# Left sums kept on chip in place of the residual: twelve of sixteen v units by seven products, and probabilities scaled by ScalarE

## The chip, the core and the metric

The kernel runs on one core of a Trainium2 chip. The core has TensorE (PE, matmuls; the loading of its stationary operand is listed apart as PEld), VectorE (DVE), ScalarE (ACT), GpSimd (POOL) and SyncE (SP). Each engine carries out its own instructions in the order in which the program wrote them and waits for the others on semaphores. On-chip data lie in SBUF, matmul results in PSUM, which here is handed out as four pairs of banks. Transfers from and to the HBM are issued by SP, and some by POOL and ACT.

The metric is the device time of one execution in microseconds; lower is better. A line such as L1074 is a line of the kernel before.

## What is computed

A decoder of two layers for 256 tokens of 2048 channels, all in float32. Layer 0 is a pooling mixer and a convolutional feed-forward part. Layer 1 is an attention whose keys and values are computed from the stream after layer 0, and another feed-forward part. Each part is followed by a layer normalisation of a scaled residual plus the part's output. What the change touches is the attention of layer 1:

```python
k_shared = (h @ shared_w_k).reshape(B_, S, N_HEADS, HEAD_DIM)   # 16 heads of 128
v_shared = (h @ shared_w_v).reshape(B_, S, N_HEADS, HEAD_DIM)
q = (h @ w_q).reshape(B_, S, N_HEADS, HEAD_DIM)
# three causal dilated branches, merged by their softmax denominators
s = where(mask, q @ k.T / sqrt(Dh), NEG_INF)
pr = exp(s - m); den = sum(pr); o = pr @ v / den
mix = o.reshape(B_, S, D_MODEL) @ w_o
h = layer_norm(DEEPNORM_ALPHA * h + mix, ln1_g, ln1_b)
```

The kernel merges the three branches into one softmax in which the mask counts how many branches hold a key (`cnt`).

## The kernel before

**Weights as units.** The program is a list of units, each a weight block of 512 rows and up to 512 columns. `run_units` takes them in turn. Ahead of unit i it issues loads up to unit i+5 (`do_load`, on SP, into three raw buffers) and splits up to unit i+3 (`do_split`). A split writes the weight as a rounded part `wh` (ACT, L99) and a rest `wl` (DVE subtraction, L100), each in one of four buffers; products are then formed from the parts by three matmuls. After a unit's matmuls come the steps that were put off to it by `later(n, ...)`, and then the unit's own closing step. So the order of the instructions on ACT and DVE is: splits of unit i+3, steps put off to unit i, closing step of unit i.

**Eight or seven products.** A v unit in its normal form (`mk`, L255 to L257) multiplies 256 tokens by 512 rows by 512 columns with 24 matmuls of 512 columns. In the other form (`mk_seven`, L244 to L246) tokens, rows and columns are halved and seven products of halves take the place of eight (a Strassen-Winograd scheme). It is then two units, "a" with 18 and "b" with 24 matmuls of 256 columns. It needs sums of weight halves, which DVE forms in the raw buffer between the pieces of the split (`split_sums`: L120, L122, L124, with casts L119 and L113 on ACT and subtractions L121 and L114 on DVE), and sums of the halves of the left operand, the "left sums". For quarter j of the 2048 channels these are formed once by `v_sums(j)`: four DVE operations on the residual `H[j]` (L992 to L995) into a tile f, and one unit later a split of f by ACT and DVE (the lines L309 and L305). The weight halves' results are put together by `v_early` and `v_post`.

**Blocks.** The attention goes through four blocks of 512 columns (four heads each): for every block four units of k, four of q and four of v, where block 1 has its v ahead of its q. I write k0, q0, v0, k1, v1, q1 and so on, and j0 to j3 for the four quarters of channels, which are the units of a group. After v3 come the 16 units of the output projection (`add_last`). Which v units take seven products is written out in `v_group`: j3 in blocks 0 and 3, and j1 to j3 in blocks 1 and 2, eight in all.

**Scores.** When a q group ends, its result is brought to SBUF, and the steps of its block are put off by given numbers of units, two heads at a time. `scores`: two heads' scores on PE (L1055, L1056), on DVE the mask (L1059), the maximum (L1062, L1063), on ACT the exponential (L1066, four instructions), on DVE the multiplication by the counts with its sum (L1069), the reciprocal (L1071) and the scaling of the probabilities (L1074, four instructions). `blocks`: a transpose in 32x32 squares on DVE (L1080) into a tile `pb`, and one unit later 16 small DMAs, eight on SP and eight on POOL (L1093), which put the squares in their places (`pTs`). `outputs`: probabilities by v on PE (L1107, L1108) and the split of the result for the output projection (L1115, L1116).

**Buffers.** The pool `hp` has five buffers of 512 KB (tag "h"). The residual, which is wanted again after the output projection, holds four, `H[0]` to `H[3]`; the fifth serves `pb` and some others in turn. The pool `xcp` has seven buffers for split operands: the attention's input takes four, the rest are for the left sums of quarters 1 and 2 (`xsum`) and the attention's outputs (`oq`). The left sums of quarter 3 lie in small tiles here and there. A tile that finds all buffers of its tag taken waits until one is given up; the instruction that writes it waits with it, and the instructions behind that on its engine.

Of the kernel before, what the change touches and what calls it, by code (L numbers as in the profile page):

```python
# [9 lines left out]
F32 = mybir.dt.float32  # L10
F32R = mybir.dt.float32r
I32 = mybir.dt.int32
AF = mybir.ActivationFunctionType
OP = mybir.AluOpType
# [18 lines left out]
def trunk(ctx: ExitStack, tc: tile.TileContext, x, pool_w_in, pool_w_grp, pool_scale, pool_w_out,  # L33
# [267 lines left out]
    def quad_tile(nm):  # L301
        return xcp.tile([P, 4, 2, XW], F32R, name=nm, tag="xc")
# [662 lines left out]
        return vts[c][:, 0, :], vts[c][:, 1, :]  # L965

    def v_post(c):
        def post(t, ps):
            v = v_tile(c)[t]
            V.tensor_tensor(v, v, ps, OP.add)  # L970
        return post

# [9 lines left out]
        return early  # L982

    vsums = {}

    def v_sums(q, then):
        ap = pools["attn"]
        x = H[q]
        a11, a12, a21, a22 = (x[:, k::2, t * P:t * P + P] for k, t in ((0, 0), (1, 0), (0, 1), (1, 1)))
        f = hp.tile([P, 4, T], F32, name="f", tag="h") if q == 3 else ap.tile([P, 4, T], F32, name="f", tag="k")  # L990
        d = [f[:, i].rearrange("p (k t) -> p k t", k=2) for i in range(4)]
        V.tensor_tensor(d[0], a21, a22, OP.add)  # L992
        V.tensor_tensor(d[1], d[0], a11, OP.subtract)
        V.tensor_tensor(d[2], a21, a11, OP.subtract)
        V.tensor_tensor(d[3], a12, d[1], OP.subtract)  # L995

        def rest():
            if q < 3:
                t = quad_tile("xsum")
                vsums[q] = [[t[:, i, hl, :T].rearrange("p (k t) -> p k t", k=2) for hl in range(2)] for i in range(4)]  # L1000
                split_act(t, f)
                then()
                return
            w = w4("vs0").bitcast(F32R)
            z = ap.tile([P, 2, T], F32R, name="vs3", tag="vs3")
            vs = [[w[:, 0], w[:, 1]], [z[:, 0], z[:, 1]]]
            vs.append([lnp.tile([P, T], F32R, name=f"vs{nm}", tag=nm) for nm in ("S", "Q")])
            vs.append([w[:, 2], w[:, 3]])
            for i, v in enumerate(vs):
                A.copy(v[0], f[:, i])  # L1010
            for i, v in enumerate(vs):
                V.tensor_tensor(v[1], f[:, i], v[0].bitcast(F32), OP.subtract)
            vsums[q] = [[u.rearrange("p (k t) -> p k t", k=2) for u in v] for v in vs]
            then()

        later(1, rest)

    def qk_post(nm, hq):
# [3 lines left out]
        def evac(ps):  # L1022
# [9 lines left out]
                    A.copy(y, p[:, :, T:])  # L1032
                    V.tensor_tensor(y, y, p[:, :, :T], OP.add)
            if nm == "q":
                s0, b0, b1, o0, o1 = ((2, 4, 7, 8, 11), (2, 4, 7, 12, 14), (9, 11, 14, 15, 18), (2, 3, 5, 7, 8))[hq]
                later(s0, lambda: scores(hq, range(0, 2)))
                later(b0, lambda: blocks(hq, (0, 1)))
                later(s0 + 1, lambda: scores(hq, range(2, 4)))
# [2 lines left out]
                later(o1, lambda: outputs(hq, (2, 3)))  # L1041
                if hq == 0:
                    v_sums(3, lambda: None)
                    later(6, lambda: v_sums(1, lambda: v_sums(2, lambda: None)))
        return post

    def scores(hq, ms):
# [23 lines left out]
        V.reciprocal(mx[:, 0:2], mx[:, 4:6])  # L1071
        for h in range(2):
            for t, sl in parts:
                V.tensor_scalar(sf[:, h, sl], sf[:, h, sl], mx[:, t, h:h + 1], None, op0=OP.mult)  # L1074
        pr[hq, ms[0]] = two

    def blocks(hq, ms):
# [38 lines left out]
            V.tensor_tensor(o[:, :, 1, :T], both[:, :, :T], o[:, :, 0, :T].bitcast(F32), OP.subtract)  # L1116

    def v_group(hq):
        js = (0, 1, 2, 3)
        seven = {0: (3,), 1: (1, 2, 3), 2: (1, 2, 3), 3: (3,)}[hq]  # L1120
        group_tm(shared_w_v, rows4, 512 * hq, 512, xsrcs, v_post(hq),
                 seven={j: (lambda j=j: vsums[j]) for j in js if j in seven}, early=v_early(hq))

    for hq in range(4):
        x0 = hq == 0
# [3 lines left out]
        group(attn_w_q[0], rows4, 512 * hq, 512, xsrcs, qk_post("q", hq))  # L1129
        if hq != 1:  # L1130
            v_group(hq)
    add_last(attn_w_o[0], rows4, [lambda j=j: oq[j] for j in range(4)], True, 1, 0, after=to_tokens)
    marks.append(len(units))
    ffn(1)
# [139 lines left out]
```

## Time and profile before

| | us |
|---|---|
| runs | 2016.05, 2016.1, 2018.27 |
| median | 2016.1 |
| span of the profiled execution, first to last instruction | 2014.9 |
| busy in the span: PE / DVE / ACT | 2005.8 / 1734.9 / 1269.7 |
| share of the 16 DMA engines' time, main queue | 58.8% |

The profile gives no time of its own for what lies around the span of the profiled execution; the median of the runs is 1.2 us above it.

A line of the timeline gives the start in us from the span's start, the duration in us of the stretch of instructions, engine, line, operation, output and inputs, and the number of instructions; in square brackets stands how long the engine was idle ahead of it and what ended the wait. A line of the waits gives who waited for whom, and the total, the number and the longest of those waits. A line of the stretches begins with its bounds, and then has the busy time of the engines, each with its instructions, the granted clock of PE, the share of the DMA engines' time and the rate in GB/s. A line of the groups gives the instructions of one kind, their number, the busy time in us and the mean duration in ns. A line of the chain gives a start, a duration and what the end of the program waited for in that time. Matmuls overlap, so that the spacing of their starts and not their duration tells their price.

The attention's units run from 924 us (k0) to 1209 us (end of v3), and the output projection follows.

### The profile page before, as it was taken

Reading aid. Unit: us, or ns where it says so; the run is one execution under the profiler, and the core shown is the slowest. Engines: PE = TensorE matmul, PEld = TensorE weight load, DVE = VectorE, ACT = ScalarE, POOL = GpSimd, SP = SyncE. Lnnn points to the kernel's source line nnn. Section 1 sums busy time; section 2 is a strip of 40 time slices with the busy share of each in tenths; the row PEclk is TensorE's granted clock in tenths of the full one; section 3 lists DMA queues with packets and bytes.
Section 4 is the critical chain, followed back from the end, with each engine's and each line's share of the span. In section 5 each row is a group of like instructions: output and inputs, shape, how many; then the busy total and the mean of one; then the engine's idle time right before and its main releaser. Section 6 shows DMA issues by size and latency. Waiting matters only on the chain.

```text
span 2014.9 us, 31474 instructions
## 1 busy us (share of the span) xinstructions
PE 2005.8 (100%) x12760; PEld 1810.2 (90%) x12760; DVE 1734.9 (86%) x1831; ACT 1269.7 (63%) x1551; POOL 93.0 (5%) x153
## 2 busy tenths in 40 slices
PE   9999999999999999999999999999999999999999
PEld 8898988999899988889888988998899989989987
DVE  6868887999899899879896878787899899989899
ACT  6454686767766676657554445487766677667673
POOL 2000000000000000000001021000000000000000
PEclk9999999999999999999999999999999999999999
DMA  8565466666666757885465656557666756666765
GB/s 260 204 208 186 163 212 192 181 221 223 198 198 200 239 179 229 232 230 186 155 220 172 210 172 202 187 188 211 166 224 200 224 186 222 209 211 186 213 208 185
DMA packets 271297, 407.77 MB, mean 202 GB/s; under 512 B 74430, under 2 KB 85588, under 8 KB 270896
## 3 DMA queue, kind: packets, MB, share of 16 engines
q1 hardware_dynamic: 259488, 388.93, 58.8%
q0 software_dynamic: 11232, 16.18, 5.4%
q8 instruction: 100, 1.64, 0.3%
q10 hardware_dynamic: 432, 0.66, 0.1%
q14 instruction: 45, 0.37, 0.1%
HBM read 380.01 MB, written 2.10 MB: 190 GB/s over the span
## 4 chain that ended last, share of the span: by engine, by line
PE 88%; DVE 7%; ACT 2%; DMA 2%; issue 1%; SPq 0%; DVEq 0%; ACTq 0%
PE acc L180 41%; PE acc L181 21%; PE s L244 3%; PE s L246 3%; PE s L245 3%; PE acc L184 2%; PE acc L185 2%; PE acc L183 2%; PE t L246 2%; PE t L244 2%; PE t L245 2%; DVE wl L100 2%; ACT wh L99 1%; DVE wl L114 1%; DVE wl L121 1%
## 5 line engine op out<-in xcount | busy, mean ns | idle before, releaser
L180 PE MATMUL acc<-xc,wh 128*128 128x512 f32 x3264 | 1151.6, 396 | 0.0
L181 PE MATMUL acc<-xc,wl 128*128 128x256 f32 x3264 | 916.2, 281 | 0.8 <-DVE wl L100 0.8
L100 DVE TENSOR_TENSOR wl<-raw,wh 128x2048 fp32r<-128x2048 f32 (+2 forms) x304 | 654.8, 2162 | 171.0 <-ACT wh L99 163.3
L180 PEld LDWEIGHTS acc<-xc,wh 128*128 128x128 f32 x3264 | 616.1, 189 | 142.8 <-issue 0.4
L99 ACT CAST wh<-raw 128x2048 fp32r<-128x2048 f32 (+2 forms) x304 | 546.6, 1805 | 170.8 <-PE acc L180 65.7
L181 PEld LDWEIGHTS acc<-xc,wl 128*128 128x128 f32 x3264 | 615.2, 188 | 1.3 <-DVE wl L100 1.2
L113 ACT CAST wh<-raw 128x1024 fp32r<-128x1024 f32 x144 | 150.7, 1052 | 202.8 <-DVE raw L122 175.5
L114 DVE TENSOR_TENSOR wl<-raw,wh 128x1024 fp32r<-128x1024 f32 x144 | 171.8, 1221 | 11.2 <-ACT wh L113 11.2
L121 DVE TENSOR_TENSOR wl<-raw,wh 128x1536 fp32r<-128x1536 f32 x72 | 126.2, 1753 | 6.3 <-ACT wh L119 5.3
L119 ACT CAST wh<-raw 128x1536 fp32r<-128x1536 f32 x72 | 106.4, 1477 | 36.6 <-PE acc L180 26.5
L287 POOL DMA_DIRECT2D ht<-w x48 | 41.3, 1015 | 1446.4 <-DVE ht L873 720.9
L244 PE MATMUL t<-wh,g 128*128 128x256 f32 x376 | 105.8, 281 | 0.0
L246 PE MATMUL t<-wh,g 128*128 128x256 f32 x376 | 105.7, 281 | 0.0
L245 PE MATMUL t<-wl,g 128*128 128x256 f32 x376 | 105.5, 281 | 0.0
L616 ACT ACTIVATE c<-u,cv 128x256 f32<-128x256 f32 x172 | 89.5, 593 | 23.2 <-DVE f L678 16.5
L246 PE MATMUL s<-wh,xs 128*128 128x256 f32 x344 | 96.1, 279 | 0.0
L244 PE MATMUL s<-wh,xs 128*128 128x256 f32 x344 | 95.9, 279 | 0.0
L245 PE MATMUL s<-wl,xs 128*128 128x256 f32 x344 | 95.9, 279 | 0.0
L124 DVE TENSOR_TENSOR raw<-raw 128x1024 f32<-128x1024 f32 x72 | 88.2, 1225 | 2.4
L621 ACT ACTIVATE a<-u,cv 128x256 f32<-128x256 f32 x172 | 73.5, 500 | 11.9 <-DVE g L688 11.9
L607 ACT COPY u<-acc 128x512 f32<-128x512 f32 x84 | 46.8, 572 | 46.1 <-PE acc L181 45.9
L621 ACT ACTIVATE u<-u,cv 128x256 f32<-128x256 f32 x172 | 73.4, 500 | 0.0
(338 smaller groups left out, 3443.1 us busy)
## 6 DMA issues: line engine op xcount, KB each, us to landing
raw<-in_ffn_w_up_dram SPq DMA_DIRECT2D x160, 1024.0 KB, 5.2
raw<-in_ffn_w_down_dram SPq DMA_DIRECT2D x80, 1024.0 KB, 5.1
raw<-in_pool_w_out_dram SPq DMA_DIRECT2D x16, 1024.0 KB, 5.0
raw<-in_shared_w_k_dram SPq DMA_DIRECT2D x16, 1024.0 KB, 5.2
raw<-in_attn_w_q_dram SPq DMA_DIRECT2D x16, 1024.0 KB, 5.3
raw<-in_shared_w_v_dram SPq DMA_DIRECT2D x16, 1024.0 KB, 5.4
raw<-in_attn_w_o_dram SPq DMA_DIRECT2D x16, 1024.0 KB, 5.2
ht<-w POOLq DMA_DIRECT2D x50, 256.0 KB, 4.8
```

The lines of the kernel that those rows point to most:

```text
L99: A.copy(wh[i][:, s], r[:, s])
L100: V.tensor_tensor(wl[i][:, s], r[:, s], wh[i][:, s].bitcast(F32), OP.subtract)
L113: A.copy(h[:, :, n], r[:, :, n])
L114: V.tensor_tensor(l[:, :, n], r[:, :, n], h[:, :, n].bitcast(F32), OP.subtract)
L119: A.copy(hs, rs)
L121: V.tensor_tensor(ls, rs, hs.bitcast(F32), OP.subtract)
L180: PE.matmul(ps[m].ap, h[:, k, c], q[:, k, :, :T], start=st, stop=False)
L181: PE.matmul(ps[m][:, :T], l[:, k, c], q[:, k, 0, :T], start=False, stop=sp)
L244: PE.matmul(to, xh, h[:, k, n], start=opens and kk == 0, stop=False)
L245: PE.matmul(to, xh, l[:, k, n], start=False, stop=False)
L246: PE.matmul(to, xl, h[:, k, n], start=False, stop=ends and kk == 1)
L621: A.activation(to[:, m, :], u[:, m, i:i + T], AF.Copy, scale=cv[:, i, j:j + 1])
```

## The change

- The residual goes to HBM while the attention runs: four transfers out when q0 ends (`parked`), four back ahead of the first unit of the output projection (`back`).
- The four buffers thus given up hold the left sums of quarters 0 and 1, two each (rounded part and rest). Those of quarter 2 stay in `xcp`, those of quarter 3 where they were. `v_sums` is now formed for quarter 0 too, in the order 0, 1, 2, beginning one unit earlier.
- Seven products: j3 in block 0, all four in blocks 1 and 2, j0, j1 and j3 in block 3, twelve in all. Block 3 takes its quarters in the order 2, 0, 1, 3.
- `v_post` adds 256 columns where all four units of a group take seven products.
- The outputs of block 3 come two units later in the list, which has two more units there.
- The four scalings of the probabilities (L1074) go from DVE to ACT.

```diff
@@ v_post
-        def post(t, ps):
-            v = v_tile(c)[t]
+        def post(t, ps, half=0):
+            v = v_tile(c)[t][:, 256 * half:]
             V.tensor_tensor(v, v, ps, OP.add)
@@ before v_sums
+    aside = ctx.enter_context(tc.tile_pool(name="aside", bufs=1, space=bass.MemoryType.DRAM))
+    parked = [aside.tile([P, 4, T], F32, name=f"parked{c}") for c in range(4)]
+
+    def back():
+        for c in range(4):
+            H[c] = hp.tile([P, 4, T], F32, name="h", tag="h")
+            nc.sync.dma_start(H[c], parked[c])
@@ v_sums
             if q < 3:
-                t = quad_tile("xsum")
-                vsums[q] = [[t[:, i, hl, :T].rearrange("p (k t) -> p k t", k=2) for hl in range(2)] for i in range(4)]
-                split_act(t, f)
+                if q == 2:
+                    t = quad_tile("xsum")
+                    t = [t[:, :, hl, :T] for hl in range(2)]
+                else:
+                    t = [hp.tile([P, 4, T], F32R, name=f"xsum{hl}", tag="h") for hl in range(2)]
+                vsums[q] = [[u[:, i].rearrange("p (k t) -> p k t", k=2) for u in t] for i in range(4)]
+                A.copy(t[0], f)
+                V.tensor_tensor(t[1], f, t[0].bitcast(F32), OP.subtract)
                 then()
@@ qk_post
-                s0, b0, b1, o0, o1 = ((2, 4, 7, 8, 11), (2, 4, 7, 12, 14), (9, 11, 14, 15, 18), (2, 3, 5, 7, 8))[hq]
+                s0, b0, b1, o0, o1 = ((2, 4, 7, 8, 11), (2, 4, 7, 12, 14), (9, 11, 14, 15, 18), (2, 3, 5, 9, 10))[hq]
@@
                 if hq == 0:
                     v_sums(3, lambda: None)
-                    later(6, lambda: v_sums(1, lambda: v_sums(2, lambda: None)))
+                    for c in range(4):
+                        nc.sync.dma_start(parked[c], H[c])
+                    later(5, lambda: v_sums(0, lambda: v_sums(1, lambda: v_sums(2, lambda: None))))
@@ scores
             for t, sl in parts:
-                V.tensor_scalar(sf[:, h, sl], sf[:, h, sl], mx[:, t, h:h + 1], None, op0=OP.mult)
+                A.activation(sf[:, h, sl], sf[:, h, sl], AF.Copy, scale=mx[:, t, h:h + 1])
@@ v_group
-        js = (0, 1, 2, 3)
-        seven = {0: (3,), 1: (1, 2, 3), 2: (1, 2, 3), 3: (3,)}[hq]
-        group_tm(shared_w_v, rows4, 512 * hq, 512, xsrcs, v_post(hq),
-                 seven={j: (lambda j=j: vsums[j]) for j in js if j in seven}, early=v_early(hq))
+        js = (2, 0, 1, 3) if hq == 3 else (0, 1, 2, 3)
+        seven = {0: (3,), 1: (0, 1, 2, 3), 2: (0, 1, 2, 3), 3: (0, 1, 3)}[hq]
+        group_tm(shared_w_v, [rows4[j] for j in js], 512 * hq, 512, [xsrcs[j] for j in js], v_post(hq),
+                 seven={i: (lambda j=j: vsums[j]) for i, j in enumerate(js) if j in seven}, early=v_early(hq))
@@ ahead of the output projection
+    before.setdefault(len(units), []).append(back)
     add_last(attn_w_o[0], rows4, [lambda j=j: oq[j] for j in range(4)], True, 1, 0, after=to_tokens)
```

## The prediction

> **What bounds the kernel now.** I read the head of the page, then the waits of the run, then the attention stage by stretches.
>
> ```profile
> span 2014.9 us, 31474 instructions
> PE 2005.8 (100%) x12760; PEld 1810.2 (90%) x12760; DVE 1734.9 (86%) x1831; ACT 1269.7 (63%) x1551; POOL 93.0 (5%) x153
> PE acc L183 <- ACT wh L99: 1.6, 1, 1.6
> PE acc L181 <- DVE wl L100: 0.8, 1, 0.8
> ```
>
> PE has matmuls in flight in all but 9 us, and no wait of it is longer than 1.6 us: a microsecond taken from its work is won, a microsecond it must wait is lost. Its one wait in attention is the 0.8 us. Its place, and the busy time of the engines in four stretches (PE, PEld, DVE, ACT, POOL, then clock and DMA):
>
> ```profile
> 1041.19 0.38 PE L181 MATMUL acc<-xc,wl 128*128 128x256 f32 x1 [0.84 <-DVE wl L100]
> ...
> 969.08:1041.13 72.05, 71.27 (x432) 63.15 (x430) 69.23 (x98) 39.69 (x42) 9.11 (x16) 1.00 0.54 163
> 1041.13:1111.28 70.15, 70.09 (x399) 61.33 (x400) 50.75 (x65) 30.04 (x28) 8.95 (x16) 1.00 0.63 199
> 1111.28:1134.34 23.06, 23.06 (x169) 21.76 (x168) 19.62 (x18) 14.26 (x12) 0.08 (x1) 1.00 0.67 222
> ...
> 1183.23:1208.86 25.63, 25.63 (x141) 22.11 (x140) 19.81 (x39) 10.35 (x17) 2.98 (x6) 1.00 0.48 168
> ```
>
> The first stretch runs from late k0 to the first unit of q1 (block 0's v, k1, v1). DVE is busy 69.2 of its 72.05 us there, and at its end PE waits for DVE: DVE, not PE, sets that point, so what is added to DVE's row of work before it comes out at the end. Elsewhere DVE has slack.
>
> **What a seven saves.** The first matmuls of a normal v unit and of what follows it, then of a seven (a and b) and of what follows it:
>
> ```profile
> 1111.28 0.40 PE L255 MATMUL t<-wh,xc 128*128 128x512 f32 x1
> 1116.88 0.28 PE L244 MATMUL s<-wh,xc 128*128 128x256 f32 x1
> ...
> 1203.78 0.47 PE L244 MATMUL s<-wh,xc 128*128 128x256 f32 x1
> 1208.86 0.39 PE L180 MATMUL acc<-o,wh 128*128 128x512 f32 x1
> ```
>
> 5.60 against 5.08 us (42 matmuls at the spacing of 0.12 us): 0.5 us a unit, 2.1 us for four. That is all the change can take from PE.
>
> **Stage A, block 0's scores to q1: DVE gets longer.** First the scaling. DVE and ACT around the first scores of block 0:
>
> ```profile
> 986.26 1.50 ACT L1066 ACTIVATE p<-p,mx 128x128 f32<-128x128 f32 x4 [3.38 <-DVE mx L1063]
> 987.66 1.89 ACT L99 CAST wh<-raw 128x2048 fp32r<-128x2048 f32 x1
> ...
> 988.25 0.18 DVE L1071 RECIPROCAL mx<-mx 128x4 f32<-128x4 f32 x1
> 988.47 1.01 DVE L1074 TENSOR_SCALAR p<-p,mx 128x128 f32<-128x128 f32 x4
> 989.58 2.29 DVE L100 TENSOR_TENSOR wl<-raw,wh 128x2048 fp32r<-128x2048 f32 x1
> ...
> L621 ACT ACTIVATE a<-u,cv 128x256 f32<-128x256 f32 x172 | 73.5, 500 | 11.9 <-DVE g L688 11.9
> ```
>
> Now ACT casts the next weights (L99) while DVE finishes the scores, and DVE's subtraction starts as both are done, at 989.58. Each engine keeps the order of the program, and the four scalings stand ahead of that cast on ACT. They wait for the reciprocal (988.43). Their price on ACT is not in the trace: the exponentials, four of the same shapes, take 1.40 us from start to cast; four at L621's 0.50 (a copy with a scale from memory, twice the width of half of them) would be 2.0; DVE's own 1.01 is the low end. I take 1.40. Then the cast runs 989.85 to 991.75, and the subtraction behind it starts 2.2 us later than now; DVE idles meanwhile. Block 0 has two such calls: **+4.4 us**. A gain (the 1.1 us of L1074 twice) would need the cast ahead of the scalings.
>
> The Trainium skill, "ScalarE: Activation LUTs", section "Rules for kernel authors", gives multiplications to VectorE rather than ScalarE. The rows side with it (1.01 on DVE, 1.50 for ACT's four of those shapes), and by it alone the sum would lose only what ACT is slower; the order on ACT, which it does not speak of, is the larger part.
>
> Then the new left sums, and the seven of v1's first unit:
>
> ```profile
> 1007.66 0.42 DVE L992 TENSOR_TENSOR f<-h 128x256 f32<-128x256 f32 x1
> ...
> 1009.12 2.29 DVE L100 TENSOR_TENSOR wl<-raw,wh 128x2048 fp32r<-128x2048 f32 x1
> 1011.33 0.97 DVE L1080 STREAM_TRANSPOSE pb<-p 128x768 f32<-128x768 f32 x1
> 1012.22 1.19 DVE L305 TENSOR_TENSOR xsum<-f,xsum 128x1024 fp32r<-128x1024 f32 x1
> ...
> 1024.37 0.68 DVE L120 TENSOR_TENSOR raw<-raw 128x512 f32<-128x512 f32 x1
> 1024.98 1.75 DVE L121 TENSOR_TENSOR wl<-raw,wh 128x1536 fp32r<-128x1536 f32 x1
> 1026.76 0.69 DVE L122 TENSOR_TENSOR raw<-raw 128x512 f32<-128x512 f32 x1
> ...
> 1028.63 2.42 DVE L114 TENSOR_TENSOR wl<-raw,wh 128x1024 fp32r<-128x1024 f32 x2
> 1030.97 0.69 DVE L1116 TENSOR_TENSOR o<-o 128x512 fp32r<-128x512 f32 x1
> ```
>
> v_sums(0) adds four operations (1007.66 to 1009.12, **+1.5**) and a low part like L305 (**+1.2**). A normal unit costs DVE 2.2 us (1009.12 to 1011.33), a seven 6.6 (1024.37 to 1030.97): **+4.4**.
>
> Then a wait. hp has five buffers: four hold the residual and one turns the transposed probabilities (pb). With the change the sums of quarters 0 and 1 take two each. When xsum1's low half is to be written, the five hold xsum0 (two), xsum1's high half, H[2] and the pb just written one DVE instruction earlier; H[2] goes only with v_sums(2), which comes after. So DVE waits until pb's 16 DMAs have landed. For the pb of the first heads:
>
> ```profile
> 999.57 0.97 DVE L1080 STREAM_TRANSPOSE pb<-p 128x768 f32<-128x768 f32 x1
> 1000.61 5.29 SPq L1093 DMA_DIRECT2D pTs<-pb  x8
> 1005.31 4.04 DMA pTs<-pb
> ```
>
> From 1000.54 to the last landing at 1009.35 it is **+8.8 us**, behind which v_sums(2) and all later weight splits stand. The low bound is nothing, if a buffer comes free otherwise.
>
> DVE's 2.8 us of idleness in the stretch lie mostly in the score chains, which stay; I let 0.6 of them cover something. Sum: 4.4 + 1.5 + 1.2 + 4.4 + 8.8 - 0.6 = **+19.7 us** at q1's start. PE's saving there is swallowed; it waits instead, mostly before v1's b units. By the end of q1 DVE is ahead again (50.8 busy of 70.2 us).
>
> **Stage B, v2 with four sevens.** DVE gets 4.4 us more in a stretch with 3.4 to spare, but it enters three units ahead, as now; the scores of block 1, 2.2 us later each, fall where it has slack. **-0.5 us**; if the lead is short, up to +1.5.
>
> **Stage C, v3.** Now three normal units stand ahead of the only seven (j2 of them between block 3's two score calls), and DVE has split that seven before the scores begin. After it one normal unit is followed by three sevens; the scores still come two and three units after q3, but a seven counts as two units, so they fall after the first a and the first b, and in program order DVE's splits for the third seven stand behind them. PE's outputs, PE's scores, and the rows of DVE and ACT that price it:
>
> ```profile
> 1182.00 0.59 PE L1107 MATMUL o<-pTs,vt 128*128 128x256 f32 x2
> 1183.23 0.48 PE L255 MATMUL t<-wh,xc 128*128 128x512 f32 x1
> ...
> 1184.95 1.50 ACT L119 CAST wh<-raw 128x1536 fp32r<-128x1536 f32 x1
> ...
> 1194.45 0.38 PE L1055 MATMUL s<-k,q 128*128 128x128 f32 x2
> 1195.57 0.59 PE L255 MATMUL t<-wh,xc 128*128 128x512 f32 x1
> ...
> 1195.96 0.96 DVE L1059 SCALAR_TENSOR_TENSOR p<-s,negm 128x768 f32<-128x768 f32 x1 [3.35 <-PE s L1056]
> 1200.20 0.18 DVE L1071 RECIPROCAL mx<-mx 128x4 f32<-128x4 f32 x1
> ```
>
> On the clock of before: PE starts j2 at 1183.2; with 5.6 for it, 2.1 for an a (18 matmuls), 1.2 for outputs and 1.1 for scores it is done with the first score call at 1193.3. Then b (24 matmuls, 2.9), scores, a, b, a: it wants the last b at 1204.4. DVE takes 0.2 after the scores to start and 4.4 to their reciprocal (1195.96 to 1200.38): 1198.0. Scaling 1.4 and cast 1.5 on ACT, L121 1.75: 1202.7. L122 and L124 of that split 1.9, the transpose of the first heads 0.9: 1205.5. Second scores 4.4: 1209.9. Scaling 1.4, half a cast 0.95 (of 1.89), half of L114's pair 1.2: 1213.5. So PE waits **9 us** for the last b, which ends at 1216.4. The first weights of the output projection come behind it (second half of the cast 0.95, a cast 1.89, a subtraction of 2.2: 1217.5), and that projection starts at about 1217.4, not 1208.9: **+8.5 us**, with the two sevens' saving in it. With the scalings on DVE the wait would be 2.6 less. The busy times alone (19.8 of 25.6 us) would not tell this; the order does.
>
> **What is hidden.** Writing the residual out: 2 MB on SP's queue behind a load of 1024 KB. They are issued as q0 ends (about 970), and a buffer is first wanted after v_sums(0) (1009): over 30 us. Fetching it back is first used four units, 22 us, into the output projection.
>
> ```profile
> raw<-in_attn_w_q_dram SPq DMA_DIRECT2D x16, 1024.0 KB, 5.3
> h<-cs POOLq DMA_DIRECT2D x2, 512.0 KB, 11.8
> ```
>
> At 5.3 us a MB each is 10.6 us, at 11.8 a piece one after the other 47; I take the first, of the same queue, so nothing on the path. If the cover went, resid_last would wait for what is over 22 us. The halved last addition of v saves a part of one short DVE operation in two groups, and the new order of v3, the later turn of block 3's outputs and xsum2's place issue nothing more: nothing.
>
> **The sum.** +19.7 - 0.5 + 8.5 = +27.7 us on the span of 2014.9, so 2042.6; the median of the runs shown, 2016.1, is 1.2 above the span, so **2043.8**.
>
> **Rivals.**
> - No buffer wait: -8.8, 2035.0. For it: the buffers are assigned by a program I only follow by hand. Against: the chain already runs from pTs' landing to the next pb. Chance 0.14.
> - DVE is through block 3's scores in time: -9.5 (two sevens' saving of 1.0 in place of +8.5), 2034.3. Chance 0.08.
> - The scaling relieves DVE (cast not behind it): -6.6 in A, -2.6 in C, 2034.6. Chance 0.07.
> - PE slows after idling: run at half rate behind its 9 us of waiting, the last b of v3 takes 2.9 us more, of which 1.0 lies beside the wait for the projection's first weights; in A DVE sets the pace. 2045.7. The granted clock is 1.00 in every stretch above, but no wait there exceeds 1.6 us, so the trace can't say. Chance 0.08. The Trainium skill, "TensorE: Matmul & The Clock Gate", "Part 1: The HAM clock gate", has such a rule: half rate after an idle window of about 3.4 us, until as much work has passed; by its figures an estimate of 1.7 us. No run here shows it.
> - Faster: DVE's additions in A find room, and PE's 2.1 us and the present 0.8 us come off: 2013.2. It needs 11 us of slack before 1041; the row shows 2.8. Chance 0.05.
> - The additions and savings cancel within 4 us, 2016: chance 0.03.
> - My forecast: 0.55.
>
> About 0.2%, 4 us, is what can be told from no change. Faster 0.05, same 0.03, slower 0.92. The range takes in the three cases near 2034 and the first two of them together (2025.5), and above ACT's dearer scaling (0.6 a call), B's 1.5 and the clock: **2025 to 2049**.
>
> **What would show it.** 72 matmuls more (12832); L1074 under ACT; PE waits of some 20 us in all between 1000 and 1065, the longest after L1080's second call; DVE idle about 9 us at xsum with pTs<-pb as its end; L99 behind the scalings; one PE wait of 8 to 9 us in the last v group. No such waits, or a matmul stream without gaps up to the output projection, would prove me wrong.

## The result, and the profile after

| | before | after |
|---|---|---|
| median of the runs on one chip, us | 2016.99 (4 runs) | 2049.45 (2047.39 to 2051.37, 4 runs) |
| ratio, 95% interval | | 1.0162 (1.0150 to 1.0174) |
| span of the profiled execution, us | 2014.9 | 2048.3 |

The changed kernel is 32.5 us slower. The forecast was 27.7 us more, 2043.8, with a range up to 2049: the sign was right, the time lies 0.45 us above the range, and a stretch that the forecast had put at nothing cost 4.1 us. Single executions that took far longer than the others of their kernel (one each of before_act, four_undone_back, eleven_back and of the kernel before) are left out of all medians and ratios below. In the changed kernel the lines of the attention have other numbers: the scaling is L1088 (L1074 before), the transposes L1094, the moves of the squares L1107, scores L1069 and L1070, outputs L1121 and L1122 with the split in L1129 and L1130, the left sums L999 to L1002 with the low part in L1013, the fetching back L991.

The head of the page of the kernel after:

```profile
span 2048.3 us, 31668 instructions
...
PE 2014.0 (98%) x12832; PEld 1818.9 (89%) x12832; DVE 1746.1 (85%) x1824; ACT 1288.6 (63%) x1592; POOL 93.1 (5%) x153
```

The 72 additional matmuls are there, PE is no longer at 100%, and its busy time has grown by 8 us although it has less to compute: some of its matmuls ran slower. Where it waited, from the waits of PE in the kernel after:

```profile
PE t L244 <- DVE o L1130: 10.0, 1, 10.0
PE s L244 <- ACT wh L113: 7.4, 1, 7.4
PE acc L181 <- DVE wl L100: 2.7, 2, 1.8
PE s L1069 <- DVE vt L981: 2.2, 1, 2.2
```

Before, no wait was longer than 1.6 us. The same stretches as in the prediction (the first runs from late q0, not k0, to the end of PE's wait in q1's first unit, the others are cut at PE's first matmul of a part), with two more (k3 and q3; the output projection up to the first step of its normalisation), in the kernel after (bounds, length, PE, PEld, DVE, ACT, POOL, clock, DMA share, GB/s):

```profile
969.00:1060.80 91.80, 76.44 (x455) 67.56 (x454) 74.02 (x99) 46.15 (x54) 9.13 (x16) 0.93 0.47 151
1060.80:1131.03 70.23, 70.06 (x399) 61.31 (x400) 47.87 (x57) 32.52 (x36) 7.10 (x13) 1.00 0.59 197
1131.03:1153.46 22.43, 22.43 (x186) 22.22 (x185) 22.17 (x23) 14.26 (x13) 1.95 (x4) 1.00 0.57 175
1153.46:1206.42 52.96, 50.76 (x282) 44.19 (x281) 38.29 (x51) 24.70 (x31) 9.08 (x16) 0.97 0.66 205
1206.42:1241.46 35.04, 26.96 (x177) 24.87 (x176) 25.78 (x43) 17.38 (x26) 4.52 (x8) 0.85 0.32 91
1241.46:1272.93 31.47, 30.98 (x178) 26.82 (x177) 21.65 (x22) 12.97 (x10) 4.53 (x8) 1.00 0.96 321
```

The clock is 0.85 to 0.97 in just the three stretches in which PE waits. Set beside the kernel before, cut at the same instructions (v0 to q1 from the first matmul of v0; starts from the timeline):

| from the start of ... to that of ... | before | after | difference | forecast |
|---|---|---|---|---|
| program, v0 | 969.98 | 970.95 | +1.0 | 0 |
| v0, q1 (A) | 69.97 | 88.73 | +18.8 | +19.7 |
| q1, v2 | 71.33 | 71.35 | 0.0 | 0 |
| v2, k3 (B) | 23.06 | 22.43 | -0.6 | -0.5 |
| k3, v3 | 48.89 | 52.96 | **+4.1** | **0** |
| v3, output projection (C) | 25.63 | 35.04 | +9.4 | +8.5 |
| output projection, its normalisation | 30.84 | 31.47 | +0.6 | 0 |
| the rest of the span | 775.2 | 775.4 | +0.2 | 0 |

The sum, 33.4, is the difference of the spans. The first row is no effect of the change: nothing of it lies there, and over the profiled runs below that point fell between 969.3 and 971.8. The profiled execution (2050.32 us) was also 0.9 us above the median of the four.

**Stage A in the timeline of the kernel after:**

```profile
989.18 0.18 DVE L1085 RECIPROCAL mx<-mx 128x4 f32<-128x4 f32 x1
...
989.39 1.49 ACT L1088 ACTIVATE p<-p,mx 128x128 f32<-128x128 f32 x4 [0.71 <-DVE mx L1085]
990.79 1.89 ACT L99 CAST wh<-raw 128x2048 fp32r<-128x2048 f32 x1
...
992.72 2.29 DVE L100 TENSOR_TENSOR wl<-raw,wh 128x2048 fp32r<-128x2048 f32 x1 [3.36 <-ACT wh L99]
...
1021.43 0.97 DVE L1094 STREAM_TRANSPOSE pb<-p 128x768 f32<-128x768 f32 x1
1029.79 1.22 DVE L1013 TENSOR_TENSOR xsum<-f,xsum 128x1024 fp32r<-128x1024 f32 x1 [7.39 <-DMA pTs<-pb]
...
1034.79 0.68 DVE L1130 TENSOR_TENSOR o<-o 128x512 fp32r<-128x512 f32 x1
...
1035.52 0.58 PE L244 MATMUL t<-wh,xc 128*128 128x256 f32 x1 [10.03 <-DVE o L1130]
```

The two mechanisms are to be read off directly. The cast stands behind the scalings on ACT, and DVE's subtraction starts 3.36 us after the reciprocal's end instead of 1.15 (988.43 to 989.58 before): 2.2 us, as forecast, and with the 1.40 us from the scalings' start to the cast that I had taken. Behind the transpose DVE stands still for 7.4 us (forecast 8.8) and then writes the low part of quarter 1's sums. The subtraction of the outputs (L1130) comes still later, and PE's first a unit of v1 cannot open its PSUM pair before that: this is PE's wait of 10.0 us. It stood in an a unit, behind its first six matmuls, not before a b unit as I had written.

**The stretch that I had at nothing, k3 and q3, in the kernel after:**

```profile
1160.60 0.69 DVE L981 TENSOR_TENSOR vt<-vt,s 128x512 f32<-128x512 f32 x1
...
1161.43 0.46 PE L1069 MATMUL s<-k,q 128*128 128x128 f32 x2 [2.20 <-DVE vt L981]
1161.73 0.61 PE L1070 MATMUL s<-k,q 128*128 128x256 f32 x2
```

The put-off numbers count units. v2 now has eight units instead of seven, but block 2's numbers were left as they were, so its first scores come after k3's first unit, no longer after its second. They need a PSUM pair that v2 still holds until DVE has put the halves together (L979 to L981). DVE is also later with that. In the kernel before:

```profile
1137.39 0.69 DVE L981 TENSOR_TENSOR vt<-vt,s 128x512 f32<-128x512 f32 x1
...
1145.56 0.38 PE L1055 MATMUL s<-k,q 128*128 128x128 f32 x2
```

There L981 ended 3.7 us after k3's first matmul (1134.34), and the scores began at 11.2 us; in the kernel after L981 ended at 7.8 us, and PE, through k3's first unit at about 5.8, waited.

### The profile page after: what moved, and what is told of

Same layout as the page of the kernel before. It is cut to its first block, busy times and chain, and to the rows that moved or that the text cites. A ratio compares the mean times of both kernels' runs of the same rounds, so it can differ in the third digit from the quotient of the medians.

```text
span 2048.3 us, 31668 instructions
## 1 busy us (share of the span) xinstructions
PE 2014.0 (98%) x12832; PEld 1818.9 (89%) x12832; DVE 1746.1 (85%) x1824; ACT 1288.6 (63%) x1592; POOL 93.1 (5%) x153
## 4 chain that ended last, share of the span: by engine, by line
PE 87%; DVE 7%; DMA 2%; ACT 2%; issue 1%; SPq 0%; POOL 0%; DVEq 0%; ACTq 0%; POOLq 0%
PE acc L180 40%; PE acc L181 20%; PE s L246 3%; PE s L245 3%; PE s L244 3%; PE acc L184 2%; PE acc L185 2%; PE acc L183 2%; PE t L244 2%; PE t L246 2%; PE t L245 2%; DVE wl L100 2%; PE t L255 1%; PE t L256 1%; PE t L257 1%
## 5 line engine op out<-in xcount | busy, mean ns | idle before, releaser
L100 DVE TENSOR_TENSOR wl<-raw,wh 128x2048 fp32r<-128x2048 f32 (+2 forms) x300 | 646.1, 2160 | 188.6 <-ACT wh L99 185.4
L99 ACT CAST wh<-raw 128x2048 fp32r<-128x2048 f32 (+2 forms) x300 | 539.0, 1804 | 160.7 <-PE acc L180 59.8
L113 ACT CAST wh<-raw 128x1024 fp32r<-128x1024 f32 x152 | 158.9, 1053 | 209.1 <-DVE raw L122 192.5
L114 DVE TENSOR_TENSOR wl<-raw,wh 128x1024 fp32r<-128x1024 f32 x152 | 181.1, 1220 | 13.2 <-ACT wh L113 13.2
L121 DVE TENSOR_TENSOR wl<-raw,wh 128x1536 fp32r<-128x1536 f32 x76 | 133.1, 1752 | 8.0 <-ACT wh L119 6.8
L119 ACT CAST wh<-raw 128x1536 fp32r<-128x1536 f32 x76 | 112.2, 1476 | 36.6 <-PE acc L180 23.7
L124 DVE TENSOR_TENSOR raw<-raw 128x1024 f32<-128x1024 f32 x76 | 93.1, 1225 | 2.6
L621 ACT ACTIVATE a<-u,cv 128x256 f32<-128x256 f32 x172 | 73.5, 499 | 11.9 <-DVE g L688 11.9
```

The lines of the kernel that those rows point to most:

```text
L99: A.copy(wh[i][:, s], r[:, s])
L100: V.tensor_tensor(wl[i][:, s], r[:, s], wh[i][:, s].bitcast(F32), OP.subtract)
L113: A.copy(h[:, :, n], r[:, :, n])
L114: V.tensor_tensor(l[:, :, n], r[:, :, n], h[:, :, n].bitcast(F32), OP.subtract)
L119: A.copy(hs, rs)
L121: V.tensor_tensor(ls, rs, hs.bitcast(F32), OP.subtract)
```

## The experiments

A table of the stretches in all profiled runs comes first; the runs are told one by one behind it. All lengths are between PE's first matmuls, in us.

| run | v0 to q1 | v2 | k3, q3 | v3 | projection | span |
|---|---|---|---|---|---|---|
| before | 69.97 | 23.06 | 48.89 | 25.63 | 30.84 | 2014.9 |
| after | 88.73 | 22.43 | 52.96 | 35.04 | 31.47 | 2048.3 |
| scale_dve | 84.37 | 22.44 | 49.91 | 32.23 | 31.39 | 2037.1 |
| sums_021 | 81.29 | 22.37 | 53.12 | 34.88 | 31.87 | 2040.4 |
| block2_later | 88.76 | 22.43 | 48.89 | 34.91 | 30.85 | 2043.1 |
| v3_as_before | 88.82 | 22.43 | 51.41 | 25.62 | 42.88 | 2049.5 |
| v3_back_later | 88.84 | 22.44 | 51.50 | 25.62 | 35.51 | 2039.9 |
| four_undone | 76.85 | 22.36 | 48.89 | 25.64 | 37.35 | 2027.3 |
| four_undone_back | 76.84 | 22.36 | 48.89 | 25.63 | 31.16 | 2020.7 |
| before_act | 75.34 | 23.05 | 48.89 | 25.64 | 35.27 | 2023.9 |
| nine_back | 69.86 | 22.44 | 48.90 | 25.64 | 30.83 | 2013.9 |
| eleven_back | 69.91 | 22.44 | 49.54 | 27.59 | 41.13 | 2030.3 |

q1 takes 71.3 us in every one of them except before_act (70.3).

### The scalings back on DVE

```diff
-                A.activation(sf[:, h, sl], sf[:, h, sl], AF.Copy, scale=mx[:, t, h:h + 1])
+                V.tensor_scalar(sf[:, h, sl], sf[:, h, sl], mx[:, t, h:h + 1], None, op0=OP.mult)
```

> The changed kernel with the four scalings of the probabilities back on DVE. Theory: the scalings hold up the cast behind them on ACT, so that DVE's next subtraction comes 2.2 us later at each call; back on DVE, block 0's two calls give 4.4 us before q1, block 3's two calls 2.5 to 4 us in v3, and the split for q3 that came late behind block 1's scores up to 2 us more: 7 to 10 us less, a ratio to before of 1.011 to 1.013; L99 stands ahead of the scalings again and DVE's idle time ahead of L100 in block 0's score calls goes from 3.4 to about 1.1 us. Rival (ACT took work off DVE, and the losses are elsewhere): the same time or up to 4 us more, 1.016 to 1.018.

Measured: 2039.87 us, ratio to before 1.0115 (1.0099 to 1.0131), 11.2 us less of span than the changed kernel. From the timeline of scale_dve:

```profile
987.53 1.89 ACT L99 CAST wh<-raw 128x2048 fp32r<-128x2048 f32 x1
...
988.13 0.18 DVE L1085 RECIPROCAL mx<-mx 128x4 f32<-128x4 f32 x1
988.34 1.01 DVE L1088 TENSOR_SCALAR p<-p,mx 128x128 f32<-128x128 f32 x4
989.45 2.29 DVE L100 TENSOR_TENSOR wl<-raw,wh 128x2048 fp32r<-128x2048 f32 x1
```

The cast is under way before the reciprocal, and L100 follows the scaling without an idle stretch. Stage A gains 4.36 us (forecast in the prediction for two calls: 4.4), v3 2.8, k3 and q3 3.0: DVE is through L981 6.3 us after k3's first matmul instead of 7.8, PE waits 0.7 us instead of 2.2, and the granted clock stays at 1.00. The rival, a relieved DVE, is out: work was taken from the fuller engine, and the time rose.

### The left sums in another order

```diff
-                    later(5, lambda: v_sums(0, lambda: v_sums(1, lambda: v_sums(2, lambda: None))))
+                    later(5, lambda: v_sums(0, lambda: v_sums(2, lambda: v_sums(1, lambda: None))))
```

> The changed kernel with the left sums formed in the order 0, 2, 1, so that H[2] is given up before the low part of quarter 1 is written. Theory: DVE's wait of 7.4 us at that low part was for a buffer held by the transposed probabilities; it goes, PE's wait of 10.0 us in v1 falls to about 3, q1 starts 7 us earlier, and the whole is 7 us shorter (ratio to before 1.0125 to 1.013). Rival (PE's 10 us hang on the landing of the moved probabilities anyway, since the outputs of block 0 use them): DVE's wait goes, but PE still waits 8 to 10 us and the time changes by less than 2 us (1.015 to 1.016).

Measured: 2042.6 us, 1.0127 (1.0111 to 1.0143). From the timeline of sums_021:

```profile
1020.12 0.97 DVE L1094 STREAM_TRANSPOSE pb<-p 128x768 f32<-128x768 f32 x1
1021.02 1.18 DVE L1013 TENSOR_TENSOR xsum<-f,xsum 128x1024 fp32r<-128x1024 f32 x1
```

and from its waits:

```profile
PE o L1121 <- DVE k L1045: 1.5, 1, 1.5
PE t L244 <- DVE o L1130: 1.3, 1, 1.3
```

With H[2] given up first the low part follows the transpose at once, and A is shorter by 7.4 us, which is what DVE's wait had been. So the wait was for a buffer; the landing of the moves themselves holds up nothing.

### Block 2's scores one unit later

```diff
-                s0, b0, b1, o0, o1 = ((2, 4, 7, 8, 11), (2, 4, 7, 12, 14), (9, 11, 14, 15, 18), (2, 3, 5, 9, 10))[hq]
+                s0, b0, b1, o0, o1 = ((2, 4, 7, 8, 11), (2, 4, 7, 12, 14), (10, 12, 15, 16, 19), (2, 3, 5, 9, 10))[hq]
```

> The changed kernel with all five put-off numbers of block 2 one unit higher, so that its scores come after the same unit of k3 as in the kernel before (v2 has one more unit now). Theory: the 4.1 us that k3 and q3 take longer (53.0 against 48.9) come from scores placed one unit earlier: PE's scores wait 2.2 us for a PSUM pair held until DVE has put block 2's v together, the next split is late by 1.8 us, and the clock is low after it; all of it goes: 48.9 us for k3 and q3, 4 us less in all (1.014). Rival (DVE is late there because of the fourth seven in v2 and the scalings, wherever the scores stand): PE's wait at the scores goes, but the wait for wl stays or grows: 51 to 53 us, 0 to 2 us less (1.015 to 1.016).

Measured: 2045.36 us, 1.0141 (1.0125 to 1.0157). k3 and q3 in a window of block2_later:

```profile
1152.46:1201.35 48.89, 48.89 (x281) 42.88 (x280) 37.45 (x50) 23.74 (x29) 7.39 (x14) 1.00 0.62 200
```

PE is busy without a gap, and the stretch is what it was before the change, to the hundredth. So the missed 4.1 us hang on the place of the scores: one unit later nothing is lost, with four sevens in v2 and the scalings on ACT. But the place is not the whole cause. At the early place scale_dve loses only 1.0 us, so the other 3.0 (half of it the clock, last section) need the scalings as well. And the fourth seven makes DVE late: in nine_back (below), which has it and the scalings on DVE, L981 ends 6.2 us after k3's first matmul, against 3.7 before. From these figures it is an estimate that the early place with DVE as early as before (3.7 against 5.8) would have cost nothing; no run has that. One part of the expectation was misread: the wait of 1.8 us for L100 lies in k1, not here. What stands beside the wait of 2.2 us in the kernel after is the clock (last section).

### v3 as before, and the residual's way back

```diff
-        js = (2, 0, 1, 3) if hq == 3 else (0, 1, 2, 3)
+        js = (0, 1, 2, 3)
-        seven = {0: (3,), 1: (0, 1, 2, 3), 2: (0, 1, 2, 3), 3: (0, 1, 3)}[hq]
+        seven = {0: (3,), 1: (0, 1, 2, 3), 2: (0, 1, 2, 3), 3: (3,)}[hq]
@@ qk_post, block 3's numbers
-(2, 3, 5, 9, 10)
+(2, 3, 5, 7, 8)
```

> The changed kernel with v3 as in the kernel before (only its last quarter by seven products, 36 matmuls fewer, quarters in the order 0 to 3, its outputs after two and three units); the scalings stay on ACT. Theory: the 35.0 us of v3 come from block 3's score calls falling between the sevens; they fall back to 25.6 (at most 26.5, since the scalings still delay two casts), the wait of 7.4 us for L113 goes, and the whole is 8.5 to 9.4 us shorter (1.0115 to 1.012). Rival (the scalings on ACT are what makes the splits late in v3, whatever its units are): v3 keeps a wait of 3 us or more for a split, 28 to 31 us, 4 to 7 us less (1.0128 to 1.0143).

Measured: 2050.39 us, 1.0162 (1.0144 to 1.0180), no gain at all; theory and rival both missed. v3 and the projection, in windows of v3_as_before:

```profile
1205.65:1231.27 25.62, 25.62 (x141) 22.12 (x139) 15.62 (x24) 9.34 (x14) 0.16 (x1) 1.00 0.40 127
1231.27:1274.15 42.88, 35.20 (x179) 30.02 (x178) 27.34 (x35) 17.52 (x19) 8.87 (x16) 0.88 0.77 238
```

v3 is whole again, and the projection has lost 12.0 us. Its timeline (PE, then SP's queue):

```profile
1238.22 0.50 PE L180 MATMUL acc<-o,wh 128*128 128x512 f32 x1 [1.17 <-ACT wh L99]
...
1240.54 0.58 PE L181 MATMUL acc<-o,wl 128*128 128x256 f32 x1 [1.83 <-DVE wl L100]
...
1259.20 1.19 PE L1121 MATMUL o<-pTs,vt 128*128 128x256 f32 x2 [4.67 <-DMA pTs<-pb]
...
1243.14 2.28 SPq L991 DMA_DIRECT2D h<-parked  x4
1245.52 11.87 SPq L1107 DMA_DIRECT2D pTs<-pb  x8
```

Two things come to light. The score calls of block 3 with the scaling on ACT now hold up the projection's second unit instead of v3's last. And the four transfers of the residual stand on SP ahead of the moves of the last probabilities: the eight moves take 11.9 us from first issue to last, and PE waits for them at the outputs. In the changed kernel the order is the other way round, because v3 has two units more there and the moves, put off by units, come before the projection's first unit. The next run fetches the residual back behind the moves:

```diff
-    before.setdefault(len(units), []).append(back)
+    before.setdefault(len(units) + 1, []).append(back)
```

> v3 as in the kernel before, as in the run v3_as_before, and the residual fetched back one unit later, behind the moves of block 3's second probabilities on SP's queue; the scalings stay on ACT. In v3_as_before v3 took 25.6 us again, but the first three units of the output projection and the outputs after them took some 10 us more (starting at 1231.27, j2 ending at 1259.2). Theory: about half of that is the 2 MB of the residual, issued ahead of those moves (their eight transfers on SP took 11.9 us instead of 5.8) and ahead of weights; the other half is the two scalings on ACT, 2.2 us each. So the wait of 4.7 us for pTs goes, PE still waits 3 us or so in j1: 4 to 6 us less than v3_as_before (ratio to before 1.0135 to 1.0142). Rival (the scalings alone): less than 1.5 us off, 1.0155 to 1.0162.

Measured: 2043.17 us, 1.0133 (1.0116 to 1.0149). SP's queue in v3_back_later:

```profile
1241.40 7.18 SPq L1107 DMA_DIRECT2D pTs<-pb  x8
...
1249.27 2.24 SPq L991 DMA_DIRECT2D h<-parked  x4
```

The wait for pTs falls from 4.67 to 0.85 us, and the projection takes 35.5 instead of 42.9 us: 7.4 us were the place of the transfers. The 4.7 that remain over before I put down to the scalings: before_act, below, has 4.4 at the same place.

### The parts together

four_undone has the edits of the four runs scale_dve, sums_021, block2_later and v3_as_before in one kernel, four_undone_back the way back of v3_back_later besides.

```diff
+                V.tensor_scalar(sf[:, h, sl], sf[:, h, sl], mx[:, t, h:h + 1], None, op0=OP.mult)
+                    later(5, lambda: v_sums(0, lambda: v_sums(2, lambda: v_sums(1, lambda: None))))
+                s0, b0, b1, o0, o1 = ((2, 4, 7, 8, 11), (2, 4, 7, 12, 14), (10, 12, 15, 16, 19), (2, 3, 5, 7, 8))[hq]
+        js = (0, 1, 2, 3)
+        seven = {0: (3,), 1: (0, 1, 2, 3), 2: (0, 1, 2, 3), 3: (3,)}[hq]
@@ four_undone_back
-    before.setdefault(len(units), []).append(back)
+    before.setdefault(len(units) + 1, []).append(back)
```

> Four parts undone together: scalings on DVE, left sums in the order 0, 2, 1, block 2's numbers one higher, v3 as in the kernel before; the residual is fetched back where the change put it. What stays is the left sums of quarter 0, v1 and v2 with four sevens each, and the residual in HBM. Theory: the parts add up: from v0's start to q1 76 to 78 us (88.7 less 4.4 and 7.4; 70.0 in the kernel before), k3 and q3 48.9, v3 25.6, v2 22.4, and the output projection still loses 4 to 6 us to the residual's transfers: 11 to 13 us over before (1.0055 to 1.0065). Rival (the residual's transfers are hidden and the projection lost its time to the scalings alone): 6 to 7.5 us over before, 1.003 to 1.0037.

> As four_undone, with the residual fetched back one unit later, behind the moves of block 3's second probabilities. Theory: the projection's 4 to 6 us go, the rest stays: 6 to 8 us over before (1.003 to 1.004), all of it ahead of q1. Rival (the transfers cost wherever they are issued, since they are 2 MB beside the weights): 9 us or more over before, 1.0045 to 1.0065.

Measured: four_undone 2028.77 us, 1.0061 (1.0046 to 1.0076), and four_undone_back 2022.60 us, 1.0028 (1.0017 to 1.0039). The parts add up: A is 76.85, which is 88.73 less 4.4 and 7.4, within 0.1. The residual's transfers cost 6.2 us of the projection in the first (37.35 against 31.16) and 0.3 in the second. What is left in four_undone_back is stage A, 6.9 us over before, in a window of it:

```profile
969.35:1046.19 76.84, 72.23 (x445) 65.13 (x443) 73.89 (x107) 40.75 (x45) 9.14 (x16) 0.96 0.53 166
```

DVE is busy 73.9 of 76.8 us and still sets the pace; the additional sums and the split of the seven were put at 1.5 + 1.2 + 4.4 - 0.6 = 6.5.

### The scalings alone, in the kernel before

```diff
-                V.tensor_scalar(sf[:, h, sl], sf[:, h, sl], mx[:, t, h:h + 1], None, op0=OP.mult)
+                A.activation(sf[:, h, sl], sf[:, h, sl], AF.Copy, scale=mx[:, t, h:h + 1])
```

> The kernel before with one part of the change alone: the four scalings of the probabilities on ACT. Theory: the scalings hold up the next cast, and DVE's next subtraction, by 2.2 us at every score call; where DVE or the split sets the pace that comes out whole: block 0 (two calls) 4.4 us before q1, block 3 (two calls) 4.4 to 4.7 us in the first units of the output projection; block 1's and block 2's calls cost up to 2 us together. In all 8.5 to 11 us more than before, ratio 1.0042 to 1.0055. Rival (DVE gains the 1.0 us of the scalings wherever it sets the pace, and the order on ACT matters only in the changed kernel, with its longer DVE row): within 2 us of before, 0.999 to 1.001.

Measured: 2025.47 us, 1.0042 (1.0027 to 1.0057): A and q1 together 4.35 us more, the projection 4.4 more, nothing in the other stretches. In before_act the subtraction after the first reciprocal:

```profile
988.37 0.18 DVE L1071 RECIPROCAL mx<-mx 128x4 f32<-128x4 f32 x1
...
991.91 2.29 DVE L100 TENSOR_TENSOR wl<-raw,wh 128x2048 fp32r<-128x2048 f32 x1 [3.36 <-ACT wh L99]
```

The 3.36 us are those of the changed kernel. The loss is the order on ACT by itself, and needs no longer DVE row. In the projection it consists of waits of 0.55 and 1.83 us and, for the rest, of a lower clock after them (0.50 from 1222.6 to 1226.0).

### Zero matmuls in the wait of v3

```diff
@@ blocks, once
+            ST["zz"] = pools["attn"].tile([P, P], F32R, name="zz", tag="zz")
+            A.activation(ST["zz"], ident, AF.Copy, scale=0.0)
@@ mk_seven, ahead of the products of v3's last b
+                    for i in range(60):
+                        PE.matmul(ps[3][:, 256:], ST["zz"], x[:, i % 4, 0, :T], start=False, stop=False)
```

> The changed kernel with 60 additional matmuls by a tile of zeros (128x256, they add nothing to the sums) ahead of the last b unit of v3, where PE waits 7.4 us for L113. Theory: the spacing of 0.21 us instead of 0.12 in that b unit is the lower clock after the wait; with PE kept busy the clock stays at 1.00 in 1232 to 1240, the b unit has spacings of 0.12 from its start, and v3 ends 0.5 to 2 us earlier (the projection's first weights, split at about 1240.5, may set its end). Rival (the slow b unit is its weights arriving piece by piece, not the clock): spacing and end of the b unit as in the changed kernel, granted clock aside.

Measured in a single execution: 2049.65 us, and v3 33.4 us instead of 35.0. Two neighbours of the b unit in the timeline of the kernel after, and the window around it:

```profile
1237.81 0.41 PE L245 MATMUL s<-wl,vs 128*128 128x256 f32 x1
1238.02 0.41 PE L246 MATMUL s<-wh,vs 128*128 128x256 f32 x1
```

```profile
1236.00:1240.00 4.00, 3.32 (x15) 3.03 (x16) 3.61 (x3) 4.00 (x3) 0.00 (x0) 0.50 0.17 26
```

The same in fill60, where the line numbers are three higher:

```profile
1237.10 0.28 PE L247 MATMUL s<-wh,vs 128*128 128x256 f32 x1
1237.22 0.28 PE L248 MATMUL s<-wl,vs 128*128 128x256 f32 x1
```

```profile
1236.00:1240.00 4.00, 3.30 (x25) 2.98 (x26) 3.60 (x4) 3.31 (x2) 0.00 (x0) 1.00 0.37 114
```

Spacing 0.21 and a clock of 0.50 without the zeros, 0.12 and 1.00 with them, on the same weights: the slow b was the clock. From its first matmul to the projection's first it takes 4.04 instead of 5.72 us. But the projection then takes 33.2 us instead of 31.5, with waits of 0.64 and 0.61 us for DVE that the kernel after doesn't have there: v3 and projection together take 66.6 us, against 66.5. By the end of the projection nothing of the gain is left, in the one execution that there is.

### Versions without the losses

```diff
@@ v_sums: quarter 0 formed in q1, its f in hp; quarters 1 and 2 in xcp as before
-        f = hp.tile([P, 4, T], F32, name="f", tag="h") if q == 3 else ap.tile([P, 4, T], F32, name="f", tag="k")
+        f = hp.tile([P, 4, T], F32, name="f", tag="h") if q in (0, 3) else ap.tile([P, 4, T], F32, name="f", tag="k")
-                if q == 2:
+                if q > 0:
-                    later(5, lambda: v_sums(0, lambda: v_sums(1, lambda: v_sums(2, lambda: None))))
+                    later(6, lambda: v_sums(1, lambda: v_sums(2, lambda: None)))
+                    later(18, lambda: v_sums(0, lambda: None))
@@ v_group
-1: (0, 1, 2, 3)
+1: (1, 2, 3)
@@ qk_post, block 3's numbers in eleven_back
-(2, 3, 5, 9, 10)
+(4, 6, 7, 9, 10)
```

Both have besides the edits of scale_dve, block2_later and v3_back_later's way back; nine_back has v3 as before, eleven_back keeps its three sevens.

> The changed kernel with all of its losses taken out: scalings on DVE, v1 with three sevens and v3 with one as in the kernel before, the left sums of quarter 0 formed in q1 instead of v0 (into the buffers that the residual gave up), those of quarters 1 and 2 in the places of the kernel before, block 2's numbers one higher, the residual fetched back behind the last moves. What stays of the change is v2's fourth seven and the residual in HBM. Theory: v0's start to q1 70.0 us, v2 22.4 (0.6 less than before), the projection up to 0.3 us more: 0.2 to 0.6 us faster than before, not to be told from it (0.9995 to 1.0). Rival (2 MB out and 2 MB back cost time wherever they run): 3 us or more slower, 1.0015 or more, with the loss in k1, v1 or the projection.

> As nine_back, but v3 with its three sevens (quarters in the order 2, 0, 1, 3) and block 3's scores two units later, after the units 4 and 5 of v3, so that the splits of all three sevens stand ahead of them; its probabilities are turned after the units 6 and 7, its outputs as in the changed kernel. Theory (the position of the scores among the splits makes v3 slow, not the sevens): v3 about 24.5 us without a wait for L113, and the whole 0.5 to 1.5 us faster than before (0.9992 to 0.9998), if the first weights of the projection are split in time. Rival (DVE has not the time for three sevens, two score calls and the projection's first weights in 25 us, wherever the scores stand): PE waits 3 us or more in v3 or in the first two units of the projection, 1.0005 to 1.003.

Measured: nine_back 2015.48 us (11 runs), 0.9993 (0.9984 to 1.0002). That is the fastest of all medians, but not to be told from the kernel before; its trace shows the 0.6 us of v2's fourth seven, and 2 MB out and back at no cost that could be seen (projection 30.83 us, 30.84 before). So with the right places the residual's room can be had for nothing, and what it bought here is 0.6 us for the one seven more that DVE could split in time.

eleven_back 2029.88 us, 1.0065 (1.0052 to 1.0079): my theory fell, the rival's figure was passed. v3 and the first two units of the projection, in windows of eleven_back:

```profile
1185.01:1212.60 27.59, 24.95 (x178) 22.97 (x176) 20.10 (x34) 12.29 (x15) 0.00 (x0) 1.00 0.45 153
1212.60:1232.42 19.82, 13.77 (x64) 11.05 (x65) 18.85 (x29) 9.07 (x9) 7.51 (x14) 0.91 0.60 158
```

and its waits, of DVE and PE:

```profile
DVE o L1131 <- ACT o L1130: 11.7, 2, 9.8
...
PE o L1122 <- DMA pTs<-pb: 4.1, 1, 4.1
```

DVE idles 9.8 us in v3, ahead of the split of block 2's outputs, and is then busy 18.9 of 19.8 us while PE waits. So the sevens of v3 cost time with the scores early (32.2 us for v3 in scale_dve) and with the scores late. Whether the outputs of block 2, placed elsewhere as well, would give DVE those 9.8 us was not tried.

## Why the prediction came out as it did

- **What bounds the kernel**: right. What was added to DVE's row of work in stage A came out at q1, and what was taken from DVE by the scalings did not count.
- **Stage A, +19.7, measured +18.8**: right in mechanism and nearly in size. The scaling's 2 x 2.2 us are 4.36 by scale_dve and 4.35 by before_act. The Trainium skill, "ScalarE: Activation LUTs", "Rules for kernel authors", would have kept the multiplication on VectorE, and the trace agrees with the advice (1.49 us on ACT, 1.01 on DVE); the larger part, the order on ACT, it does not speak of. The longer row (6.5) is 6.9 by four_undone_back. The term that was off is the buffer wait, 7.4 instead of 8.8; its mechanism is shown by sums_021. That PE would wait "mostly before v1's b units" was wrong: it waits 10.0 us in an a unit, for a PSUM pair that the outputs hold. Its waits between 1000 and 1065 come to 15 us, not to "some 20".
- **Stage B, -0.5, measured -0.6**: right for the stretch itself. But the step broke off at v2's end, and **here the prediction failed**: I counted v2's units for PE and DVE and not for the numbers that put block 2's scores off. I had worked out just this for block 3 ("a seven counts as two units") and looked at block 1's scores only ("fall where it has slack"). In its place the runs showed scores that come one unit earlier and wait 2.2 us for a PSUM pair that v2 still holds, with a lower clock behind the wait: +4.1 us, all of which block2_later takes away. That block 1's later scores "fall where it has slack" failed with it: 3.0 of the 4.1 us go when the scalings are back on DVE (scale_dve), which then has L981 done 1.5 us sooner; the other half of the 3.0 is the clock. Even the range's 1.5 us for B did not cover it; with the 4.1 in the sum the forecast would have been 2047.9, 1.5 us below the 2049.45 measured. That the misses of A (-0.9) and C (+0.9) cancel is chance.
- **Stage C, +8.5, measured +9.4**: the order of events was as worked out. The scaling's share, forecast as 2.6 us, is 2.8 by scale_dve. The wait was put too high (9 us; 7.4, and 0.7 for the b unit's second weights), and the clock was missing: the b unit ran at half speed after the wait. I had that as a rival for this place, with 1.9 us and a chance of 0.08; fill60 shows a b unit longer by 1.7 us. For v3's end it is no rival but an addition, and should have stood in the sum. For the whole time it is not shown to count: in fill60 the projection ended no sooner.
- **The clock rule.** The Trainium skill, "TensorE: Matmul & The Clock Gate", "Part 1: The HAM clock gate", says half rate after an idle window, and the trace of after agrees (0.50 in the four microseconds after the wait). The estimate of 1.7 us, worked out for this place from that window, is what fill60 shows for the b unit.
- **The residual's transfers, 0**: the figure was right in the changed kernel (projection +0.6) and the reason only half right. I looked at when the residual is first used and not at what stands behind its transfers on SP. They were harmless because v3's two additional units brought the moves of the probabilities ahead of them; with v3 as before they cost 7.4 us (v3_as_before against v3_back_later), and 6.2 with the scalings on DVE.
- **Blame for v3.** That the sevens of v3 made the loss of C was too simple a reading. With v3 as before, its loss turned up in the projection: v3 and projection together take 66.5 us in the changed kernel, 68.5 with v3 as before, 61.1 with the transfers moved as well, and 56.8 with the scalings on DVE besides (four_undone_back; 56.5 before). Of the 10.0 us that the two lose, the scalings back on DVE alone give 2.9 (scale_dve, 63.6), v3 as before alone 5.4 (v3_back_later), and both 9.7: neither is the cause by itself.

## What to carry to other kernels

Where work is put off by a count of units, a change in the number of units moves every step whose count runs across it: list all of them, not those of the stage that is changed. Moving work to an emptier engine is a loss if it waits there for the fuller one and the engine's next task, which the fuller one needs, stands behind it. And a stage's loss is not known from its own stretch: undo it and see whether the time comes back at the end or turns up in the next stage.

## What the runs showed of the hardware

- The granted clock can fall after a wait of little over 2 us, and does not do so each time. The same wait of 2.2 to 2.4 us before block 2's scores was followed by half rate in three executions (after, sums_021, fill60) and by full rate in two (v3_as_before, v3_back_later). The window around that wait in the kernel after, and the one behind it in v3_as_before:

```profile
1160.00:1166.00 6.00, 4.57 (x17) 4.03 (x18) 5.86 (x9) 0.17 (x1) 0.00 (x0) 0.72 0.59 195
```

```profile
1162.00:1166.00 4.00, 3.78 (x22) 3.39 (x23) 3.96 (x5) 0.00 (x0) 0.00 (x0) 1.00 0.70 257
```

  The clock makes 1.5 us of k3 and q3 (52.96 against 51.41). The Trainium skill, "TensorE: Matmul & The Clock Gate", "Part 1: The HAM clock gate", has a window that runs freely, which would fit a result that changes from one execution to the next; by its window of about 3.4 us, however, a wait of 2.2 us could not leave a whole one idle, and here the measurement decides.
- In the kernel after, half rate lasted 3.7 and 4.9 us from PE's new start behind the waits of 10.0 and 7.4 us (1035.5 to 1039.2, 1235.7 to 1240.6); it had set in during these waits (at 1029.1 and 1230.5). Behind the wait of 2.2 us PE started at full rate at 1161.4, and half rate came 0.8 us later and lasted 3.4 us (1162.2 to 1165.6).
- Eight moves of 24 KB on SP behind 2 MB of other transfers on the same queue took 11.9 us to be issued (v3_as_before), against 7.2 when they went first (v3_back_later).
